# A two-block transformer on one core: second attention in another order, softmax joined over a step, set-up of the recurrence moved

## The chip, the cores and the metric

The kernel runs on one core of a Trainium2 chip. The metric is the device time of one execution in microseconds (us). A core has a matrix engine (TensorE, PE in the profile), a vector engine (VectorE, DVE), a scalar engine (ScalarE, ACT), a general one (GpSimd, POOL) and a queue engine for transfers (SyncE, SP). Each runs its own list of instructions strictly in order, and semaphores make one wait for another.

## The reference

256 tokens of width 1024 go through two blocks. The first block has two attention layers, each followed by a gated per-layer embedding (PLE):

```python
def first_block(x, p, ...):
    for i in range(DEPTH):                       # DEPTH = 2
        h = rms_norm(x, norm_gain[i])
        x = x + (moba_layer if i % 2 == 0 else nsa_layer)(h, ...)
        gate = jax.nn.sigmoid(rms_norm(x, ple_gate_gain[i]) @ ple_w_gate[i])
        x = x + gate * (p[i] @ ple_w_proj[i])
    return x

def nsa_layer(h, w_in, ...):
    q, kc, vc, ks, vs, kw, vw, gl, z = jnp.split(h @ w_in, offs, axis=-1)
    kc = compress(split_heads(kc, 4), cmp_pe[0], cmp_w1[0], cmp_w2[0])
    vc = compress(split_heads(vc, 4), cmp_pe[1], cmp_w1[1], cmp_w2[1])
    ...
    g = jax.nn.sigmoid(gl).reshape(B, T, N_HEADS, 3).transpose(0, 2, 1, 3)
    o = merge_heads(nsa_attention(q, kc, vc, ks, vs, kw, vw, g)) * jax.nn.silu(z)
    return o @ w_out
```

The first attention (MoBA) is plain causal attention at this length (one block of 256 keys), 16 heads of 64. The second (NSA) adds three branches for every head, each scaled by its own sigmoid gate: attention over compressed keys (`compress`: windows of 32 tokens, an MLP of width 256), over selected blocks and over a window; with 256 tokens the last two are both causal attention over all keys, with different keys and values. The second block has two layers; each starts with three mixers in parallel (a state-space recurrence `s5_mixer`, latent attention and a gated linear recurrence), then cross attention and a gated MLP. The recurrence's parameters (step sizes, complex exponentials, bounds) depend on the weights alone.

## The kernel before, in words

Everything is float32. A matrix product `x @ w` splits both operands into a high and a low part and runs three products per block of 128 rows: high by high, low by high, high by low (`dense`, L493 to L495, with the weight streaming as 512 columns; `mm_T`, L507 to L509, with the activations streaming as 256 columns). `weights` (L463 to L478) fetches a weight tile by a transfer on SP's queue, casts it to `whi` on ACT (L476) and forms `wlo` on DVE (L477). `hilo` (L394, L396, L397) does the same to activations.

Attention runs in steps (`attention`, `step`). A two-bank step takes heads of even and of odd number into two PSUM banks: products for the scores (`score`, L1003 in NSA), `softmax` for each bank (L577 to L601), transposes of the probabilities on PE with a copy on ACT (`transposed`, L610 and L612), and products with the values (L659). In `softmax`, DVE adds the mask and takes the row maximum (L587), ACT takes the exponential with its sum (L594), DVE inverts the sum (L596), multiplies it by the gate where there is one (L598) and scales the probabilities (L599). `pipeline` keeps one step in flight ahead of the next.

Work that is to lie beside dense products is a generator in a list of background jobs. `spawn(job, rate)` enters it, each weight tile of a dense product calls `tick`, which advances every job by its rate, and `finish` runs a job to its end. In this way the program's order of instructions is made; a scheduler then fixes each engine's list from it.

In `moba` (up to L758) the two halves of the heads are spawned, `swish_T` forms the gate, `ple_proj(0)` multiplies the embedding, the jobs are finished, `gated` multiplies by the gate and splits, and `project` is the output projection, whose result is added to `x` (L528). After it the main program spawns `setup_mix` at rate 0.6 (L1988) and finishes it behind `nsa`. `setup_mix` (L1895) runs `ssm_params`, `hg_bound`, `hg_reset` and `mla_tables`: small transfers on POOL's queue, transposes on PE (L1267) and a long series of DVE instructions on 128x32 tiles: an exponential by a polynomial (L1226 to L1239), reductions of angles (L1245 to L1249, L1283 to L1298) and the coefficients (L1303 to L1353).

In `nsa` the order before is: product for the compressed keys and values (`pc`), `compress_blocks`, queries and keys of half 0, gates, queries of half 1, spawn of half 0's attention, `compress_mlp` for the keys, keys of half 1, spawn of half 1's attention, `compress_keys`, `swish(0)`, `compress_mlp` for the values, `compressed` (scores of the compressed branch L974, its softmax L980 to L990), `swish(1)`, `compress_values` (L919, L922), `compressed_T` (L997), `ple_proj(1)`, the rest of the attention jobs, `blend` (L1021) and the output projection.

Of the kernel before, what the change touches and what calls it, by code (L numbers as in the profile page):

```python
# [14 lines left out]
OP = mybir.AluOpType  # L15
# [28 lines left out]
R_PREP, R_SET = (0.8, 0.4), 0.6  # L44
# [186 lines left out]
class Net:  # L231
# [345 lines left out]
    def softmax(self, own, t, heads, ps, scale, causal, gate):  # L577


        nc = self.nc  # L580
        n, nk = ps.shape[1], ps.shape[2]
        s, mx, sm = own.F(n, nk), own.T(n), own.T(n)
        if causal:
            mask = self.c["tri"][:, 256 - nk:256]
            ops, far = ((OP.add, OP.min), 3e38) if scale == -1.0 else ((OP.subtract, OP.max), -3e38)
            for i in range(n):
                nc.vector.tensor_tensor_reduce(s[:, i, :], ps[:, i, :], mask, 1.0, far, *ops, mx[:, i:i + 1])  # L587
        else:
            nc.vector.reduce_max(mx, ps, axis=AX.X)
        if scale != -1.0:  # L590
            nc.vector.tensor_scalar(mx, mx, -scale, None, op0=OP.mult)
        src = s if causal else ps
        for i in range(n):
# [21 lines left out]
    def attention(self, t, steps, score, scale, v, blocks, end, causal=True, gate=None, joint=1):  # L615
# [16 lines left out]
        def step(gs):  # L632
            own = Scope(self)

            def scores():
# [4 lines left out]
                return [self.softmax(own, t, hs, p, scale, causal, gate) for p, hs in zip(ps, gs)]  # L640

            def turn(ws):
                out = []
                for w in ws:
                    out.append(self.transposed(own, w))
                    own.drop(w)
# [62 lines left out]
    def moba(self, act):  # L709
# [39 lines left out]
        self.swish_T(act, w, 3 * D, sz)  # L749
        proj = self.ple_proj(0)  # L750
# [5 lines left out]
        nxt = self.boundary(self.project(oT, I["moba_w_out"][0], D), self.gain("ple_gate_gain", 0))  # L756
        oT.close()
# [168 lines left out]
    def nsa(self, act):  # L926
# [73 lines left out]
        def attend(g, qT):  # L1000
            def block(t, b):
# [4 lines left out]
                def end(bank):  # L1006
# [3 lines left out]
                    else:  # L1010
# [3 lines left out]
                                      gate=lambda hs: gate[:, t, hs[0]:hs[-1] + 1:2, 1 + b])  # L1014
# [30 lines left out]

        pc = self.dense(act, w, D, 1024, 512)
# [3 lines left out]
        own0, qT0 = queries(0)  # L1050
# [969 lines left out]
```

## Time and profile before

| what | value |
|---|---|
| runs | 1521.4, 1518.18, 1514.51 us; median 1518.18 us |
| profiled execution | 1515.88 us, its span 1514.1 us |
| mean granted clock of PE | 0.991 |
| busy share of the span | PE 96%, PE weight load 83%, DVE 76%, ACT 58%, POOL 3% |
| chain that ended last | PE 73%, DVE 13%, ACT 8%, transfers 3%, issue 3% |

The span reaches from the first to the last instruction of the profiled execution; 1.78 us lie around it. The chain that ended last is followed back from the last instruction, at each step to what released it. A wait is an engine's idle time before an instruction, put down to the engine that released it last. The granted clock is a share of PE's full speed: 1.0 is 2.4 GHz, 0.5 is 1.2 GHz.

### The profile page before, as it was taken

How to read it: one execution, taken by the hardware profiler on the slowest of the kernel's cores; microseconds unless marked ns; L12 is line 12 of the kernel's file. 1: busy time of each engine (PE TensorE's matmuls, PEld its weight loads, DVE VectorE, ACT ScalarE, POOL GpSimd, SP SyncE). 2: the span in 40 equal slices, each digit the busy share in tenths (PEclk: the TensorE clock that was granted, in tenths of full speed). 3: DMA queues.
4: the chain of work that ended last, by engine and by line, in shares of the span. 5: the costliest groups of instructions: out<-in, count | busy, mean ns of one | idle time of the engine just before them, and what ended most of it. 6: DMA issues, size and time to landing. Idle time of an engine off the chain costs nothing.

```text
span 1514.1 us, 25628 instructions
## 1 busy us (share of the span) xinstructions
PE 1451.9 (96%) x9781; PEld 1259.1 (83%) x9781; DVE 1146.0 (76%) x2479; ACT 881.9 (58%) x1646; POOL 45.7 (3%) x80
## 2 busy tenths in 40 slices
PE   7999999999999999999999999989899999999997
PEld 6787777876788988788889999979787888799996
DVE  7886798988999899757786765676996667665556
ACT  5665566776577966445544544568774455644443
POOL 1001000002000000000100000000000000000000
PEclk9999999999999999999999999999999999999999
DMA  6544545513444345455635555434354565356663
GB/s 201 165 141 127 176 135 177 164 38 117 158 119 137 114 140 172 137 194 169 186 112 181 181 169 182 153 117 123 98 181 140 182 208 163 121 184 202 192 183 125
DMA packets 156059, 233.31 MB, mean 154 GB/s; under 512 B 8946, under 2 KB 91680, under 8 KB 155936
## 3 DMA queue, kind: packets, MB, share of 16 engines
q1 hardware_dynamic: 153888, 228.03, 48.7%
q0 software_dynamic: 1440, 2.53, 0.8%
q8 instruction: 77, 1.26, 0.3%
q10 hardware_dynamic: 608, 1.11, 0.2%
q14 instruction: 46, 0.38, 0.1%
HBM read 230.59 MB, written 1.05 MB: 153 GB/s over the span
## 4 chain that ended last, share of the span: by engine, by line
PE 73%; DVE 13%; ACT 8%; DMA 3%; issue 3%; POOL 0%; SPq 0%; ACTq 0%; DVEq 0%; POOLq 0%
PE mm L493 11%; PE mm L494 10%; PE mm L495 10%; PE sq L507 4%; PE sq L508 4%; PE sq L509 4%; DVE wlo L477 3%; ACT whi L476 3%; PE mm L507 3%; PE mm L508 2%; PE mm L1153 2%; PE mm L1152 2%; PE mm L1154 2%; PE mm L509 2%; PE sq L407 1%
## 5 line engine op out<-in xcount | busy, mean ns | idle before, releaser
L476 ACT CAST whi<-raw 128x1024 fp32r<-128x1024 f32 (+3 forms) x442 | 439.4, 1020 | 400.7 <-PE sq L508 94.8
L477 DVE TENSOR_TENSOR wlo<-raw,whi 128x1024 fp32r<-128x1024 f32 (+3 forms) x442 | 514.1, 1184 | 181.5 <-ACT whi L476 180.2
L493 PE MATMUL mm<-whi,rslab 128*128 128x512 f32 (+1 forms) x944 | 372.0, 396 | 6.9 <-DVE tslab L379 2.9
L494 PE MATMUL mm<-whi,rslab 128*128 128x512 f32 (+1 forms) x944 | 369.6, 392 | 0.1
L495 PE MATMUL mm<-wlo,rslab 128*128 128x512 f32 (+1 forms) x944 | 366.8, 390 | 2.8 <-DVE wlo L477 2.8
L493 PEld LDWEIGHTS mm<-whi,rslab 128*128 128x128 f32 x944 | 178.4, 189 | 46.2 <-ACT whi L476 7.1
L495 PEld LDWEIGHTS mm<-wlo,rslab 128*128 128x128 f32 x944 | 178.9, 190 | 39.4 <-DVE wlo L477 5.5
L494 PEld LDWEIGHTS mm<-whi,rslab 128*128 128x128 f32 x944 | 179.1, 190 | 34.8 <-DVE rslab L397 1.5
L508 PE MATMUL sq<-rslab,whi 128*128 128x256 f32 x544 | 153.0, 281 | 1.3 <-DVE rslab L397 1.0
L507 PE MATMUL sq<-rslab,whi 128*128 128x256 f32 x544 | 153.4, 282 | 0.1
L509 PE MATMUL sq<-rslab,wlo 128*128 128x256 f32 x544 | 152.6, 281 | 0.0
L507 PE MATMUL mm<-rslab,whi 128*128 128x256 f32 x448 | 127.0, 286 | 0.3 <-ACT rslab L396 0.3
L509 PE MATMUL mm<-rslab,wlo 128*128 128x256 f32 x448 | 126.1, 282 | 0.4 <-DVE wlo L477 0.4
L508 PE MATMUL mm<-rslab,whi 128*128 128x256 f32 x448 | 125.6, 282 | 0.0
L508 PEld LDWEIGHTS sq<-rslab,whi 128*128 128x128 f32 x544 | 103.0, 189 | 2.7 <-DVE rslab L397 1.9
L507 PEld LDWEIGHTS sq<-rslab,whi 128*128 128x128 f32 x544 | 103.0, 189 | 1.6 <-ACT fslab L1442 0.7
L509 PEld LDWEIGHTS sq<-rslab,wlo 128*128 128x128 f32 x544 | 103.0, 189 | 0.0
L508 PEld LDWEIGHTS mm<-rslab,whi 128*128 128x128 f32 x448 | 84.1, 188 | 1.8 <-issue 1.1
L507 PEld LDWEIGHTS mm<-rslab,whi 128*128 128x128 f32 x448 | 83.9, 188 | 1.8 <-issue 0.7
L509 PEld LDWEIGHTS mm<-rslab,wlo 128*128 128x128 f32 x448 | 84.2, 188 | 1.2 <-DVE wlo L477 0.8
L1153 PE MATMUL mm<-whi,rslab 128*128 128x512 f32 x176 | 68.9, 391 | 0.0
L1152 PE MATMUL mm<-whi,rslab 128*128 128x512 f32 x176 | 68.8, 393 | 0.0
(448 smaller groups left out, 2288.1 us busy)
## 6 DMA issues: line engine op xcount, KB each, us to landing
raw<-in_w_in_dram SPq DMA_DIRECT2D x96, 512.0 KB, 3.8
raw<-in_ffn_w_gate_up_dram SPq DMA_DIRECT2D x88, 512.0 KB, 4.2
raw<-in_ffn_w_down_dram SPq DMA_DIRECT2D x44, 512.0 KB, 4.2
raw<-in_moba_w_in_dram SPq DMA_DIRECT2D x32, 512.0 KB, 4.5
raw<-in_nsa_w_in_dram SPq DMA_DIRECT2D x28, 512.0 KB, 3.7
raw<-in_ple_w_gate_dram SPq DMA_DIRECT2D x16, 512.0 KB, 4.4
raw<-in_ssm_w_glu_dram SPq DMA_DIRECT2D x16, 512.0 KB, 4.2
raw<-in_w_out_dram SPq DMA_DIRECT2D x16, 512.0 KB, 4.4
```

The costliest lines, as they stand in the source:

```text
L407: nc.tensor.transpose(ps[:, j, t * 128:(t + 1) * 128], src[t][:, (k + j) * 128:(k + j + 1) * 128], self.ident)
L476: nc.scalar.copy(hi[:, js], raw)
L477: nc.vector.tensor_sub(lo[:, js], raw, hi[:, js].bitcast(F32))
L493: nc.tensor.matmul(o, act.hi[:, k, ts], wh[:, j, :], start=k == 0, stop=False)
L494: nc.tensor.matmul(o, act.lo[:, k, ts], wh[:, j, :], start=False, stop=False)
L495: nc.tensor.matmul(o, act.hi[:, k, ts], wl[:, j, :], start=False, stop=k == nkb - 1)
L507: nc.tensor.matmul(o, wh[:, k, fs], act.hi[:, k, :], start=k + i == 0, stop=False, skip_group_check=True)
L508: nc.tensor.matmul(o, wh[:, k, fs], act.lo[:, k, :], start=False, stop=False, skip_group_check=True)
L509: nc.tensor.matmul(o, wl[:, k, fs], act.hi[:, k, :], start=False, stop=last, skip_group_check=True)
L1152: nc.tensor.matmul(o, mid.hi[:, j, ts], wh[:, j, ns], start=first, stop=False)
L1153: nc.tensor.matmul(o, mid.lo[:, j, ts], wh[:, j, ns], start=False, stop=False)
L1154: nc.tensor.matmul(o, mid.hi[:, j, ts], wl[:, j, ns], start=False, stop=last)
```

## The change

There are three parts. **Softmax**: `softmax` takes all banks of a step at once; the reciprocal, the gate product and the scaling are done once for both banks (one 128x1024 operation in place of two of 128x512). **Set-up**: `setup_mix` is spawned inside `moba`, between `swish_T` and `ple_proj(0)`, at rate 1.0, and finished at the end of `moba`. **Order of `nsa`**: gates, queries and keys of both halves come first and each half's attention is spawned as soon as its keys are there; the compressed branch's product, blocks, MLPs, scores and values follow, with `swish(0)` and `swish(1)` ahead of each MLP.

```diff
-R_PREP, R_SET = (0.8, 0.4), 0.6
+R_PREP, R_SET = (0.8, 0.4), 1.0
...
-    def softmax(self, own, t, heads, ps, scale, causal, gate):
+    def softmax(self, own, banks, scale, causal, gate):
...
-        n, nk = ps.shape[1], ps.shape[2]
-        s, mx, sm = own.F(n, nk), own.T(n), own.T(n)
+        m, n, nk = len(banks), banks[0].shape[1], banks[0].shape[2]
+        s, mx, sm = own.F(m, n, nk), own.T(m, n), own.T(m, n)
+        for j, ps in enumerate(banks):
...
             for i in range(n):
-            nc.scalar.activation(s[:, i, :], src[:, i, :], AF.Exp, bias=mx[:, i:i + 1], scale=scale,
-                                 accum_out=sm[:, i:i + 1])
+                nc.scalar.activation(s[:, j, i, :], src[:, i, :], AF.Exp, bias=mx[:, j, i:i + 1], scale=scale,
+                                     accum_out=sm[:, j, i:i + 1])
         nc.vector.reciprocal(sm, sm)
         if gate is not None:
-            nc.vector.tensor_mul(sm, sm, gate(heads))
-        nc.vector.tensor_mul(s, s, sm[:, :, None].to_broadcast([128, n, nk]))
+            nc.vector.tensor_mul(sm, sm, gate)
+        flat = lambda a: a.rearrange("p m n k -> p (m n) k") if len(a.shape) == 4 else a.rearrange("p m n -> p (m n)")
+        nc.vector.tensor_mul(flat(s), flat(s), flat(sm)[:, :, None].to_broadcast([128, m * n, nk]))
...
         self.swish_T(act, w, 3 * D, sz)
+        setup = self.spawn(self.setup_mix(), R_SET)
         proj = self.ple_proj(0)
...
         nxt = self.boundary(self.project(oT, I["moba_w_out"][0], D), self.gain("ple_gate_gain", 0))
+        self.finish(setup)
...
+        gate = sc.F(NT, 16, 3)
+        gates()
+        own0, qT0 = queries(0)
+        keys(0)
+        jobs = [self.spawn(attend(0, qT0), R_NSA[0])]
+        own1, qT1 = queries(1)
+        keys(1)
+        jobs.append(self.spawn(attend(1, qT1), R_NSA[1]))
         pc = self.dense(act, w, D, 1024, 512)
         s1 = Scope(self)
         kk = [self.compress_in(s1, pc, c, act) for c in range(2)]
         blocks = self.compress_blocks(kk[0], 0, pe)
-        own0, qT0 = queries(0)
-        keys(0)
-        gate = sc.F(NT, 16, 3)
-        gates()
-        own1, qT1 = queries(1)
-        jobs = [self.spawn(attend(0, qT0), R_NSA[0])]
+        swish(0)
...
         self.compress_mlp(blocks, 0, gT[0])
         blocks = self.compress_blocks(kk[1], 1, pe)
         s1.close()
-        keys(1)
-        jobs.append(self.spawn(attend(1, qT1), R_NSA[1]))
         self.compress_keys(gT[0], w2, rope[3], kcB)
-        swish(0)
+        swish(1)
         self.compress_mlp(blocks, 1, gT[1])
...
         compressed(1, qT1, pcm[1])
-        swish(1)
         self.compress_values(gT[1], w2, vbd)
...
         act, proj = net.moba(act)
-        setup = net.spawn(net.setup_mix(), R_SET)
         act = net.ple(0, act, proj, net.gain("norm_gain", 1))
         act, proj = net.nsa(act)
-        net.finish(setup)
```

Instructions on each engine: DVE has 48 fewer, PE, ACT and POOL as many as before. Line numbers of the changed file lie up to two higher (L1226 is L1228 there, L997 is L999, L612 is L614).

The change moves instructions on the engines. Ahead of the first attention's output projection, DVE's list before ran from the split of the embedding (`hilo`, L394) to the first gated operand (L397) with three weight splits between:

```order
L394 TENSOR_TENSOR rslab<-sq_1218,rslab 128x512
L477 TENSOR_TENSOR wlo_1322<-raw_1323,whi_1321 128x1024
L477 TENSOR_TENSOR wlo_1322<-raw_1327,whi_1321 128x1024
L477 TENSOR_TENSOR wlo_1356<-raw_1357,whi_1355 128x1024
L397 SCALAR_TENSOR_TENSOR rslab<-fslab,rslab 128x512 x2
L477 TENSOR_TENSOR wlo_1356<-raw_1361,whi_1355 128x1024
```

Now 79 rows stand between that L394 and the first L397 (one of them for four equal instructions); these are the last of them, set-up for the most part:

```order
L1308 TENSOR_SCALAR tslab<-tslab 128x32
L1316 TENSOR_TENSOR tslab<-tslab,ssm_prm 128x32
L1312 TENSOR_TENSOR tslab<-tslab 128x32
L1327 SCALAR_TENSOR_TENSOR fslab<-fslab 128x32
L477 TENSOR_TENSOR wlo_1489<-raw_1494,whi_1488 128x1024
L1313 RECIPROCAL tslab<-tslab 128x32
L1315 TENSOR_TENSOR tslab<-tslab,ssm_prm 128x32
L1588 TENSOR_TENSOR tslab<-tslab 128x4
L397 SCALAR_TENSOR_TENSOR rslab<-fslab,rslab 128x512
L1317 TENSOR_TENSOR tslab<-tslab 128x32
L1589 TENSOR_TENSOR hg_lbt<-tslab 128x4
L397 SCALAR_TENSOR_TENSOR rslab<-fslab,rslab 128x512
```

The 78 set-up instructions between are those of `ssm_params`, `hg_bound` and `mla_tables`, and they came behind the output projection before.

In the second attention's tail, PE's list before had the compressed branch's scores (L974) among swish's products (L507 to L509):

```order
L509 MATMUL mm_3195<-rslab,wlo_3186 128x256
L507 MATMUL mm_3195<-rslab,whi_3185 128x256
L974 MATMUL sq_3062<-fslab 128x64 x8
L974 MATMUL sq_3080<-fslab 128x64 x8
L1003 MATMUL sq_3158<-fslab 128x256
L1003 MATMUL sq_3157<-fslab 128x256
L1003 MATMUL sq_3158<-fslab 128x256
L1003 MATMUL sq_3157<-fslab 128x256
L659 MATMUL po_3177<-fslab 64x256 x4
L508 MATMUL mm_3195<-rslab,whi_3185 128x256
```

The transposes of its probabilities (L997) came 42 rows later. Now the scores (L976), the compressed values' products (L921) and the transposes (L999) follow one another, behind the last MLP, with four products of an attention step (L659) between:

```order
L612 MATMUL sq_3331<-cst,fslab 128x128 x4
L612 MATMUL sq_3337<-cst,fslab 128x128 x4
L885 MATMUL sq_3349<-cst,fslab 128x68 x2
L976 MATMUL sq_3354<-fslab 128x64 x8
L976 MATMUL sq_3372<-fslab 128x64 x8
L921 MATMUL sq_3390<-fslab 128x64
L659 MATMUL po_3449<-fslab 64x256 x4
L921 MATMUL sq_3390<-fslab 128x64 x7
L999 MATMUL sq_3405<-cst,fslab 128x128 x4
L999 MATMUL sq_3411<-cst,fslab 128x128 x4
L407 MATMUL sq_3418<-cst,fslab 128x128 x4
```

Swish's products stand ahead of all of these now.

## Rows read from the trace of the kernel before

**Rows 1.** The page: busy time of each engine, its share of the span, instructions

```profile
PE 1451.9 (96%) x9781; PEld 1259.1 (83%) x9781; DVE 1146.0 (76%) x2479; ACT 881.9 (58%) x1646; POOL 45.7 (3%) x80
```

**Rows 2.** Windows by stage: us, busy time (instructions) of each engine, granted clock, DMA

```profile
164.00:189.00 25.00, 25.00 (x119) 20.19 (x119) 20.89 (x60) 15.56 (x27) 0.00 (x0) 1.00 0.53 174
189.00:258.00 69.00, 63.86 (x320) 50.47 (x319) 63.16 (x221) 43.77 (x66) 1.12 (x4) 1.00 0.54 159
258.00:319.00 61.00, 58.66 (x443) 49.59 (x442) 55.59 (x196) 47.69 (x132) 0.17 (x1) 1.00 0.44 130
319.00:364.00 45.00, 42.72 (x279) 31.51 (x278) 38.30 (x121) 29.40 (x81) 2.80 (x3) 0.96 0.24 77
```

**Rows 3.** Windows: 180 to 240 us, columns as in rows 2

```profile
180.00:240.00 60.00, 56.50 (x270) 44.79 (x269) 58.23 (x225) 37.43 (x63) 0.95 (x2) 1.00 0.49 144
```

**Rows 4.** Timeline of DVE, 130 to 142 us: start, us, line, operation [idle before]

```profile
130.05 0.69 DVE L599 TENSOR_TENSOR fslab<-fslab,tslab 128x512 f32<-128x512 f32 x1
130.66 0.68 DVE L394 TENSOR_TENSOR rslab<-sq,rslab 128x512 fp32r<-128x512 f32 x1
135.78 2.36 DVE L477 TENSOR_TENSOR wlo<-raw,whi 128x1024 fp32r<-128x1024 f32 x2 [4.43 <-ACT whi L476]
139.14 1.22 DVE L477 TENSOR_TENSOR wlo<-raw,whi 128x1024 fp32r<-128x1024 f32 x1 [1.00 <-ACT whi L476]
140.64 1.29 DVE L397 SCALAR_TENSOR_TENSOR rslab<-fslab,rslab 128x512 fp32r<-128x512 f32 x2 [0.28 <-ACT rslab L396]
```

**Rows 5.** Timeline of PE: the first attention's output projection begins

```profile
139.64 1.10 PE L659 MATMUL po<-fslab 128*64 128x128 f32 x16 [1.00 <-ACT fslab L612]
140.67 0.73 PE L493 MATMUL mm<-whi,rslab 128*128 128x512 f32 x2
141.39 0.50 PE L494 MATMUL mm<-whi,rslab 128*128 128x512 f32 x1
```

**Rows 6.** Timeline of DVE: set-up instructions in a chain, and mixed

```profile
177.95 0.18 DVE L1226 TENSOR_SCALAR tslab<-ssm_prm 128x32 f32<-128x32 f32 x1
178.17 0.18 DVE L1227 TENSOR_SCALAR tslab<-tslab 128x32 f32<-128x32 f32 x1
...
178.71 1.22 DVE L477 TENSOR_TENSOR wlo<-raw,whi 128x1024 fp32r<-128x1024 f32 x1
179.85 0.18 DVE L1230 SCALAR_TENSOR_TENSOR tslab<-tslab 128x32 f32<-128x32 f32 x1
...
192.11 0.19 DVE L1234 SCALAR_TENSOR_TENSOR ssm_r<-ssm_r,tslab 128x32 f32<-128x32 f32 x1
...
193.59 0.18 DVE L1237 TENSOR_SCALAR ssm_r<-ssm_r 128x32 f32<-128x32 f32 x1
193.68 1.23 DVE L477 TENSOR_TENSOR wlo<-raw,whi 128x1024 fp32r<-128x1024 f32 x1
```

**Rows 7.** Windows around a PE stall, columns as in rows 2

```profile
378.00:381.00 3.00, 0.02 (x1) 0.00 (x0) 1.02 (x5) 1.05 (x2) 0.00 (x0) 1.00 0.46 153
381.00:385.00 4.00, 3.40 (x12) 3.01 (x13) 4.00 (x9) 2.07 (x6) 0.00 (x0) 0.57 0.15 38
```

**Rows 8.** Timeline of PE: the second attention's tail

```profile
318.05 3.68 PE L974 MATMUL sq<-fslab 128*128 128x64 f32 x32
...
322.72 1.08 PE L659 MATMUL po<-fslab 128*64 128x256 f32 x8
...
335.56 1.58 PE L997 MATMUL sq<-cst,fslab 128*128 128x128 f32 x8
...
338.26 1.55 PE L919 MATMUL sq<-fslab 128*128 128x64 f32 x12
```

**Rows 9.** Timeline of DVE: the compressed branch's softmax and values

```profile
322.97 1.27 DVE L982 TENSOR_REDUCE tslab<-fslab 128x16 f32<-128x512 f32 x2
324.16 1.28 DVE L983 TENSOR_TENSOR fslab<-fslab,tslab 128x512 f32<-128x512 f32 x2
...
325.70 1.27 DVE L985 TENSOR_REDUCE tslab<-fslab 128x16 f32<-128x512 f32 x2
326.89 0.37 DVE L986 RECIPROCAL tslab<-tslab 128x16 f32<-128x16 f32 x2
...
339.85 1.42 DVE L922 TENSOR_TENSOR fslab<-sq,cst 128x256 f32<-128x256 f32 x4 [0.78 <-PE sq L919]
```

**Rows 10.** Groups by form, ACT: exponentials of banks of two heads

```profile
L594 ACT ACTIVATE fslab<-fslab,tslab 128x256 f32<-128x256 f32 x64 | 31.9, 503 | 3.5 <-DVE tslab L587 3.1
```

More of the change, by code (lines that the diff above doesn't have):

```diff
@@ L575, in heads @@
         return [p[:, off:off + nh * 64].rearrange("p (h d) -> p h d", d=64) for p in ps]
-    def softmax(self, own, t, heads, ps, scale, causal, gate):
+    def softmax(self, own, banks, scale, causal, gate):
         nc = self.nc
-        n, nk = ps.shape[1], ps.shape[2]
-        s, mx, sm = own.F(n, nk), own.T(n), own.T(n)
-        if causal:
-            mask = self.c["tri"][:, 256 - nk:256]
-            ops, far = ((OP.add, OP.min), 3e38) if scale == -1.0 else ((OP.subtract, OP.max), -3e38)
-            for i in range(n):
[L587 to L593, printed above, removed]
-            nc.scalar.activation(s[:, i, :], src[:, i, :], AF.Exp, bias=mx[:, i:i + 1], scale=scale,
-                                 accum_out=sm[:, i:i + 1])
+        m, n, nk = len(banks), banks[0].shape[1], banks[0].shape[2]
+        s, mx, sm = own.F(m, n, nk), own.T(m, n), own.T(m, n)
+        for j, ps in enumerate(banks):
+            if causal:
+                mask = self.c["tri"][:, 256 - nk:256]
+                ops, far = ((OP.add, OP.min), 3e38) if scale == -1.0 else ((OP.subtract, OP.max), -3e38)
+                for i in range(n):
+                    nc.vector.tensor_tensor_reduce(s[:, j, i, :], ps[:, i, :], mask, 1.0, far, *ops, mx[:, j, i:i + 1])
+            else:
+                nc.vector.reduce_max(mx[:, j], ps, axis=AX.X)
+            if scale != -1.0:
+                nc.vector.tensor_scalar(mx[:, j], mx[:, j], -scale, None, op0=OP.mult)
+            src = s[:, j] if causal else ps
+            for i in range(n):
+                nc.scalar.activation(s[:, j, i, :], src[:, i, :], AF.Exp, bias=mx[:, j, i:i + 1], scale=scale,
+                                     accum_out=sm[:, j, i:i + 1])
@@ L639, in scores, with turn @@
                         score(p[:, i, :], hs[i], nk)
[L640 to L646, printed above, removed]
+                return self.softmax(own, ps, scale, causal, gate and gate(gs[0][0], len(gs[0])))
+            def turn(w):
+                out = [self.transposed(own, w[:, j]) for j in range(len(gs))]
+                own.drop(w)
                 return out
@@ L1013, in block @@
                                       lambda h, kb: vs[b][:, kb, h // 4, :], (4, 2), end, joint=2,
-                                      gate=lambda hs: gate[:, t, hs[0]:hs[-1] + 1:2, 1 + b])
+                                      gate=lambda h, n: gate[:, t, h:h + 2 * n, 1 + b].rearrange("p (i u) -> p u i", u=2))
             yield from self.pipeline((st for b in range(2) for t in range(NT) for st in block(t, b)), LEAD)
```

## The prediction

> **What bounds the kernel now.** I read the page first. TensorE (PE) is busy 96% of the 1514.1 us span [rows 1], so time is to be had or lost only where PE stands idle or runs at the lower clock. The change touches only the stages between the first attention's last step (about 125 us) and the second attention's output projection (about 364 us); from there on the two programs' PE orders read almost alike. So the windows of that stretch come next [rows 2]: PE is busy in all of 164 to 189 us, for 63.86 of the 69 us of the second attention's first part, for 58.66 of 61 us in its middle and for 42.72 of 45 us in its tail. Idle time is 5.1, 2.3 and 2.3 us, and the tail also has a mean granted clock of 0.96, which is 0.04 x 45 = 1.8 us more. That is all that a better order can win here: 11.5 us. In the first part VectorE (DVE) is what is full: 58.23 of 60 us between 180 and 240 [rows 3], because the set-up of the recurrence parameters runs there, over 100 small instructions.
>
> Around the first attention's output projection it is the other way round. DVE runs `hilo` (L394) at 130.66 us and then waits 4.43, 1.00 and 0.28 us before it forms the first gated operand (L397) at 140.64 us [rows 4]. The output projection's first two products, which need the high part alone, start on PE at 140.67 us, and the first that needs L397's low part (L494) at 141.39 us [rows 5]: there is no slack.
>
> **The set-up, moved.** By the order on DVE, 78 small instructions and four `wlo` splits now stand between L394 and the first L397; before there were three splits. Seven more small ones stand just ahead of L394. What one costs there is not in the trace at this place, so I bound it from where the set-up runs now [rows 6]. In a strict chain they start 0.22 us apart (177.95 to 178.17); where two or three chains are mixed, 16 of them take 1.57 us (192.11 to 193.68), 0.098 each. The new rows are mostly mixed and chained at the start, and I take a quarter at 0.22 and the rest at 0.098, so 0.13. A `wlo` takes 1.14 us from start to start (178.71 to 179.85 in the same view, and half of 2.36 us in [rows 4]). So L397 comes at 131.3 (end of L394) + 0.7 (the seven) + 78 x 0.13 + 4 x 1.14 = 146.7 us in place of 140.64: the output projection is **6.1 us late**. Bounds: with 0.098 it is 3.5 us, with 0.22 it is 13.2 us. Nothing covers it: ahead of that product PE has only the steps of the attention that it finishes anyway, and its order there has no other dense work left.
>
> An idle PE of this length has a second price. In the profile, after the 3 us in which PE did 0.02 us of work, the next 4 us have a granted clock of 0.57 [rows 7], which is mostly 1.2 GHz in place of 2.4, so 0.43 x 4 = **1.7 us**. Bounds 0 and 3.4 (twice).
>
> The set-up leaves 177 to 221 us. PE loses 5.1 us in the window that holds this [rows 2]; I take back 4.6 us of it (**-4.6**; bounds 0 and -5.1), since the first part is now dense work for queries, keys and gates with a relieved DVE. The parameters' small loads on GpSimd's queue go ahead of the second attention's gain loads; those wait behind the position load, which waits for a DVE result of the set-up. I cost this at nothing: they are needed only in the second attention. The gates' and compression weights' loads on SyncE's queue trade places with equal loads: nothing.
>
> **The second attention, reordered.** The attention steps begin earlier and lie under swish and both compression MLPs: the middle can win at most its 2.3 us. Against this DVE has to do most of the attention in that stretch, and where DVE was that full PE lost 60 - 56.50 = 3.5 us in 60 [rows 3]. I put 0 (bounds -2.3 and +4).
>
> The tail is where PE's order binds. Before, the compressed branch's scores (L974) run at 318.05 us and the transposes of its probabilities (L997) at 335.56 us [rows 8]; the 17.5 us between are filled with swish's products and attention steps. Now, by the order, PE has between them only the second half of the scores (1.84 us), the compressed values' products (2.1 us for 16 like the 12 of 1.55) and one group of four L659 (0.54 us): 4.5 us. Meanwhile DVE and ACT must do the compressed softmax for both halves [rows 9]: L980, L982, L983, L985 and L990 twice each at 0.60 from start to start (6.0), L986 and four tiny ones (0.7), two copies and four products of the values (2.0), and one joint 128x1024 product (1.2): about 10 us. PE waits the rest, **5.6 us**, at L997's successor, L999, and everything behind it waits too, as PE runs its list in order; its clock then falls as above (**1.7 us**). The old tail's 2.3 us of idle time and 1.8 us of clock go away in exchange (**-4.1**). Net **+3.2**. Bounds: -4.1 if the chain hides, +7.3 if the old waits stay.
>
> **The joint softmax.** Per two-bank step (18 of them) one reciprocal, one gate product and one scaling of 128x1024 stand for two each. Two L599 take 2 x 0.61 from start to start (130.05 to 130.66 in [rows 4]), one 128x1024 operation 1.14; with the small ones a step saves about 0.3 us of DVE, 18 x 0.3 = 5 us in all, where DVE has room nearly everywhere: I put 0 (bounds -2 and +6.4). The price is that the first bank's transposes wait for the second bank's exponentials too: two at 0.50 us each [rows 10] and half the product, 1.6 us per step, hidden while another step is in flight. The Trainium skill, "Perfetto Trace Analysis", section "Optimizing Scalar/DVE Operations", speaks against this edit here: where DVE and ScalarE are not saturated but hold up other engines, it advises smaller instructions so that work is done sooner. By that rule the sum would be higher by what the last rival below gives.
>
> **Sum.** 6.1 + 1.7 - 4.6 + 0 + 3.2 + 0 = +6.4 us. The profiled execution took 1515.88 us, so **1522.3 us**. That execution lies 2.3 us under the median of the three runs, 1518.18, and within their spread of 1514.51 to 1521.4; I add nothing for it.
>
> **The rivals.**
> A, *the cover wins* (faster). The set-up's instructions mix perfectly (3.5 us late, PE's clock stays up), the first part wins all of 5.1, the middle 2.3, and the compressed chain hides in attention steps that are late anyway, so the old tail's 4.1 goes: 3.5 - 5.1 - 2.3 - 4.1 = -8.0, 1507.9 us. For it: the second attention's dense work now surrounds all of its steps. Against it: the order in the tail, and L397 behind 78 instructions.
> B, *the set-up is a chain* (slower). DVE starts its 78 instructions 0.22 us apart: 13.2 us in place of 6.1, total +13.5, 1529.4 us. It decides the sign from 0.145 us apart on, where the sum passes +7.6. For it: the exponential's polynomial and the angle reductions are chains, each instruction reading the one before. Against it: the mixed stretch in [rows 6].
> C, *little happens*. The late L397 costs 3.5 us without a clock drop, the relief returns 4.6, the tail gives and takes the same: -1.1, 1514.8 us. That the change does not do what it says is excluded by the order, where the set-up and the compressed branch stand in their new places.
> D, *joining exposes the first bank*. In the tail's last four steps, where no step behind covers, the transposes wait 1.6 us longer each: +6.4 on top of the sum, 1528.7 us. The Trainium skill's sentence above is this mechanism. For it: in the old tail PE already waits for ACT's and DVE's softmax results. Against it: in the new tail fewer steps are left.
>
> **Chances.** A measurement of this kernel can tell about 0.5%, 7.6 us, from no change. Forecast 0.40, of which 0.17 lies above +7.6 (its sum is 1.2 us below that bound); A 0.30, of which 0.25 passes -7.6; B 0.11; C 0.14; D 0.05. So faster 0.25, within 0.5% 0.23 + 0.05 + 0.14 = 0.42, slower 0.17 + 0.11 + 0.05 = 0.33. The range reaches from 1505 (A less the 2 us that the joint softmax can give, and rounded down) to 1532 (B plus the 1.7 us by which the clock's bound lies over its value, and rounded up); about 2 in 10 lie outside.
>
> **What would show it.** In the new profile DVE has no idle time between L394 and the first L397, PE a gap of about 6 us ahead of the first attention's output projection with a lower granted clock behind it; PE is nearly full from 180 us to the first scores of the second attention; a PE wait of 5 to 6 us stands before the transposes of the compressed probabilities, in a tail without swish. If PE's order there shows no such waits, the sum is wrong by these terms; if the middle shows PE idle for more than 4 us beside a full DVE, the term that I put at 0 was the one that mattered.

## The result and the profile after

The changed kernel took 1531.54 us (median of 5 runs, 1528.80 to 1534.82) beside 1518.94 us for the kernel before (5 runs, 1514.51 to 1521.52): a ratio of 1.0085, with a 95% interval of 1.0056 to 1.0113. It is slower by 12.6 us, beyond the 0.5% that a measurement of this kernel can tell. The forecast was 1522.3 us in a range of 1505 to 1532.

The page of the changed kernel: busy time of each engine [rows 1].

```profile
PE 1457.6 (95%) x9781; PEld 1265.4 (83%) x9781; DVE 1144.9 (75%) x2431; ACT 883.1 (58%) x1646; POOL 45.6 (3%) x80
```

PE's busy time rose by 5.7 us and its idle time from 1514.1 - 1451.9 = 62.2 to 1527.0 - 1457.6 = 69.4 us. The mean granted clock over the span fell from 0.991 to 0.986: 1514.1 x 0.009 = 13.6 us were lost to the clock before, 1527.0 x 0.014 = 21.4 us now. Idle time and clock each grew by some 7 us (idle time at half rate counts in both).

DVE's timeline around the first attention's output projection, from `hilo` to the first gated operand [rows 4]:

```profile
131.51 0.69 DVE L394 TENSOR_TENSOR rslab<-sq,rslab 128x512 fp32r<-128x512 f32 x1
132.11 0.18 DVE L1232 SCALAR_TENSOR_TENSOR tslab<-tslab 128x32 f32<-128x32 f32 x1
...
136.31 1.22 DVE L477 TENSOR_TENSOR wlo<-raw,whi 128x1024 fp32r<-128x1024 f32 x1
...
144.12 1.23 DVE L477 TENSOR_TENSOR wlo<-raw,whi 128x1024 fp32r<-128x1024 f32 x1
...
145.63 0.69 DVE L397 SCALAR_TENSOR_TENSOR rslab<-fslab,rslab 128x512 fp32r<-128x512 f32 x1
```

DVE's timeline has no wait between L394 and the first L397, which starts at 145.63 us, 5.0 us later than before. PE's timeline there [rows 5]:

```profile
140.78 0.73 PE L493 MATMUL mm<-whi,rslab 128*128 128x512 f32 x2 [0.50 <-ACT rslab L396]
146.38 0.80 PE L494 MATMUL mm<-whi,rslab 128*128 128x512 f32 x1 [4.87 <-DVE rslab L397]
146.97 0.63 PE L495 MATMUL mm<-wlo,rslab 128*128 128x512 f32 x1
147.40 0.63 PE L493 MATMUL mm<-whi,rslab 128*128 128x512 f32 x1
...
152.09 0.43 PE L493 MATMUL mm<-whi,rslab 128*128 128x512 f32 x1
152.37 0.40 PE L494 MATMUL mm<-whi,rslab 128*128 128x512 f32 x1
```

PE waits 4.87 us for that operand. Behind the wait 13 products, to 152.09 us, start 0.43 us apart, and then 0.23 us. The windows of the same place and of the second attention (us, busy time and instructions of PE, PEld, DVE, ACT and POOL, granted clock, DMA) [rows 2]:

```profile
146.00:152.00 6.00, 5.62 (x13) 4.47 (x14) 6.00 (x32) 1.26 (x2) 2.88 (x5) 0.50 0.50 111
189.00:262.00 73.00, 70.81 (x350) 54.87 (x350) 60.77 (x160) 44.01 (x86) 0.00 (x0) 1.00 0.53 157
262.00:340.00 78.00, 74.45 (x572) 62.49 (x570) 65.49 (x190) 64.66 (x168) 1.64 (x5) 1.00 0.38 113
340.00:372.00 32.00, 26.84 (x160) 20.61 (x160) 22.86 (x51) 15.79 (x31) 1.90 (x2) 0.89 0.30 95
```

The first addition to `x` (L528) starts at 157.90 us in place of 151.06. From 189 to 262 us PE is idle for 2.2 of 73 us (5.1 of 69 before), with DVE at 60.77; from 262 to 340 us it is idle for 3.55 of 78 (2.3 of 61). The tail has 5.2 us idle in 32 and a clock of 0.89. PE's timeline in the tail [rows 8], in which the waits stand where the order put them:

```profile
345.49 3.79 PE L976 MATMUL sq<-fslab 128*128 128x64 f32 x32
...
352.13 1.98 PE L921 MATMUL sq<-fslab 128*128 128x64 f32 x14 [1.61 <-DVE fslab L918]
356.41 1.09 PE L999 MATMUL sq<-cst,fslab 128*128 128x128 f32 x4 [2.31 <-DVE fslab L992]
358.07 1.09 PE L999 MATMUL sq<-cst,fslab 128*128 128x128 f32 x4 [0.58 <-DVE fslab L992]
```

PE waits 1.61 us for a copy on DVE (L918) and 2.31 and 0.58 us for the compressed probabilities (L992).

### The profile page after: what moved, and what is told of

It reads as the page before. It is cut to its first block, busy times and chain, and to the rows that moved or that the text cites. A ratio compares the mean times of both kernels' runs of the same rounds, so it can differ in the third digit from the quotient of the medians.

```text
span 1527.0 us, 25580 instructions
## 1 busy us (share of the span) xinstructions
PE 1457.6 (95%) x9781; PEld 1265.4 (83%) x9781; DVE 1144.9 (75%) x2431; ACT 883.1 (58%) x1646; POOL 45.6 (3%) x80
## 4 chain that ended last, share of the span: by engine, by line
PE 70%; DVE 9%; ACT 8%; DMA 2%; issue 2%; POOL 0%; ACTq 0%; DVEq 0%; SPq 0%; POOLq 0%
PE mm L493 10%; PE mm L494 10%; PE mm L495 10%; PE sq L507 4%; PE sq L508 4%; PE sq L509 4%; ACT whi L476 3%; PE mm L1155 2%; PE mm L1154 2%; PE mm L1156 2%; PE mm L507 2%; PE mm L509 2%; PE mm L508 2%; DVE wlo L477 2%; PE sq L407 2%
## 5 line engine op out<-in xcount | busy, mean ns | idle before, releaser
L494 PE MATMUL mm<-whi,rslab 128*128 128x512 f32 (+1 forms) x944 | 369.4, 392 | 5.4 <-DVE rslab L397 5.3
L494 PEld LDWEIGHTS mm<-whi,rslab 128*128 128x128 f32 x944 | 179.2, 190 | 40.1 <-DVE rslab L397 6.7
L507 PE MATMUL sq<-rslab,whi 128*128 128x256 f32 x544 | 153.4, 282 | 0.1
L509 PE MATMUL sq<-rslab,wlo 128*128 128x256 f32 x544 | 152.6, 280 | 0.0
L507 PE MATMUL mm<-rslab,whi 128*128 128x256 f32 x448 | 128.9, 290 | 0.3 <-ACT rslab L396 0.3
L509 PE MATMUL mm<-rslab,wlo 128*128 128x256 f32 x448 | 127.2, 285 | 0.4 <-DVE wlo L477 0.4
L508 PE MATMUL mm<-rslab,whi 128*128 128x256 f32 x448 | 127.4, 286 | 0.0
L507 PEld LDWEIGHTS sq<-rslab,whi 128*128 128x128 f32 x544 | 103.0, 189 | 1.6 <-ACT fslab L1444 0.7
L509 PEld LDWEIGHTS sq<-rslab,wlo 128*128 128x128 f32 x544 | 103.0, 189 | 0.0
L507 PEld LDWEIGHTS mm<-rslab,whi 128*128 128x128 f32 x448 | 85.4, 192 | 2.3 <-issue 1.2
L509 PEld LDWEIGHTS mm<-rslab,wlo 128*128 128x128 f32 x448 | 85.7, 191 | 1.6 <-DVE wlo L477 1.2
L508 PEld LDWEIGHTS mm<-rslab,whi 128*128 128x128 f32 x448 | 85.7, 192 | 1.5 <-issue 0.7
L1155 PE MATMUL mm<-whi,rslab 128*128 128x512 f32 x176 | 68.9, 391 | 0.0
L1156 PE MATMUL mm<-wlo,rslab 128*128 128x512 f32 x176 | 68.8, 391 | 0.0
```

Source lines behind the costliest of these rows:

```text
L494: nc.tensor.matmul(o, act.lo[:, k, ts], wh[:, j, :], start=False, stop=False)
L507: nc.tensor.matmul(o, wh[:, k, fs], act.hi[:, k, :], start=k + i == 0, stop=False, skip_group_check=True)
L508: nc.tensor.matmul(o, wh[:, k, fs], act.lo[:, k, :], start=False, stop=False, skip_group_check=True)
L509: nc.tensor.matmul(o, wl[:, k, fs], act.hi[:, k, :], start=False, stop=last, skip_group_check=True)
L1155: nc.tensor.matmul(o, mid.lo[:, j, ts], wh[:, j, ns], start=False, stop=False)
L1156: nc.tensor.matmul(o, mid.hi[:, j, ts], wl[:, j, ns], start=False, stop=last)
```

## The experiments

The three parts of the change could be taken apart, except that the new order was not tried without the joint softmax. In the table, x1 and x2 are the starts of the first addition to `x` (L528) of the first and second attention, from each run's profile; the median has 6 to 12 runs (before: 5, changed: 5), and the ratio is to runs of the kernel before on the same chip. The runs were spread over several chips, so ratios are compared below, and medians of two rows only with care.

| run | median us | ratio and interval | x1 | x1 to x2 | x2 to end |
|---|---|---|---|---|---|
| before | 1518.94 | | 151.06 | 223.50 | 1139.5 |
| changed | 1531.54 | 1.0085 (1.0056 to 1.0113) | 157.90 | 223.55 | 1145.6 |
| e1 joint softmax alone | 1520.20 | 1.0011 (0.9992 to 1.0031) | 151.60 | 225.90 | 1141.0 |
| e2 set-up alone | 1520.19 | 1.0015 (0.9998 to 1.0033) | 154.66 | 223.13 | 1137.4 |
| e3 without the set-up's move | 1525.70 | 1.0049 (1.0034 to 1.0064) | 154.88 | 228.35 | 1138.3 |
| e4 set-up behind the gated products | 1519.72 | 1.0014 (0.9998 to 1.0030) | 149.87 | 224.97 | 1143.0 |
| e5 compressed scores early | 1525.16 | 1.0051 (1.0032 to 1.0071) | 159.03 | 223.76 | 1140.5 |
| e6 e4 and e5 together | 1521.17 | 1.0015 (1.0000 to 1.0029) | 151.25 | 224.87 | 1143.3 |
| e7 before, with e4's set-up | 1516.92 | 0.9985 (0.9970 to 1.0001) | 150.37 | 220.29 | 1139.9 |
| e8 PE kept busy in the wait | 1531.21 | 1.0080 (1.0057 to 1.0102) | 159.52 | 223.87 | 1145.2 |
| e9 e4, second swish late | 1525.28 | 1.0030 (1.0011 to 1.0048) | 149.71 | 231.31 | 1142.3 |
| e10 e7 with the joint softmax | 1518.12 | 0.9994 (0.9976 to 1.0013) | 150.09 | 223.97 | 1137.8 |
| e11 changed kernel again | 1530.85 | 1.0069 (1.0047 to 1.0092) | 158.53 | 223.73 | 1142.8 |
| e12 e7 again | 1517.97 | 0.9989 (0.9974 to 1.0005) | 150.22 | 221.20 | 1140.0 |

**e1, the joint softmax alone.**

```diff
...
-                return [self.softmax(own, t, hs, p, scale, causal, gate) for p, hs in zip(ps, gs)]
+                return self.softmax(own, ps, scale, causal, gate and gate(gs[0][0], len(gs[0])))
...
```

The rest of the edit is the new body of `softmax`, as in the change.

> The kernel before with the joint softmax alone (set-up and order of the second attention as before). My theory, that DVE's saving of about 5 us lies beside other work and that a step in flight hides the longer wait: within 3 us of before, no new PE wait above 1 us. The rival that joining exposes the first bank's transposes: 4 to 7 us slower, with longer PE waits at the transposes in the second attention's bare tail (327 to 335 us). The rival that a relieved DVE pays: 2 to 5 us faster.

The ratio is 1.0011, 1.7 us, and its interval takes in 1. My theory holds for the time; not for the waits, since a new one of 1.7 us appears (L919 behind L916). Whether joining costs a little, the interval leaves open.

**e2, the set-up alone.**

```diff
-R_PREP, R_SET = (0.8, 0.4), 0.6
+R_PREP, R_SET = (0.8, 0.4), 1.0
...
         self.swish_T(act, w, 3 * D, sz)
+        setup = self.spawn(self.setup_mix(), R_SET)
...
+        self.finish(setup)
...
-        setup = net.spawn(net.setup_mix(), R_SET)
...
-        net.finish(setup)
```

> The kernel before with the set-up alone moved into the first attention. My theory (the first gated operand stands behind the set-up on DVE, PE waits 5 us and then runs at half clock): about 7 us later at the first x update, 3 to 4 us given back in the second attention's first part where DVE is relieved, so 3 to 4 us slower in all. The rival that the whole loss of the changed kernel comes from the second attention's new order: within 1 us of before or faster.

1.0015, some 2 us, below the 3 to 4 expected. x1 is 3.6 us late, not 7: beside the old softmax 52 small instructions and three splits stand ahead of the first L397 on DVE, where the changed kernel has 78 and four; it starts at 143.07 us, 2.6 us earlier than there, and PE's longest wait for an L397 is 1.7 us. The stage behind x1 is 0.4 us shorter. So this part costs, but alone it costs only about a sixth of the 12.6 us (0.0015 x 1518 = 2.2).

**e3, the changed kernel without the set-up's move** (the diff of e2 taken back).

> The changed kernel with the set-up put back behind the first attention (joint softmax and new order kept). My theory: the first x update is back at 151 us; the set-up fills DVE again while the second attention's first dense products run; the tail's wait at the transposes of the compressed probabilities (2.3 + 0.6 us in the changed kernel) and its low clock stay: 3 to 6 us slower than before, 7 to 9 us faster than the changed kernel. The rival that the new order alone costs it all: as slow as the changed kernel, 12 us over before.

1.0049, 7.4 us over before and 5.5 us (1.0085 - 1.0049) below the changed kernel: between my theory and the rival, and nearer to mine. The stage from x1 to x2 takes 228.35 us, 4.85 more than before. With e1 at 1.0011, the new order costs some 0.0038, 5.8 us, when nothing relieves DVE. x1 was to be back at 151 us and came at 154.88, 3.3 us later than in e1, though the lists of PE, DVE and ACT are the same in both up to the second attention. The reason is in the windows, of e3:

```profile
130.00:137.00 7.00, 5.92 (x24) 4.11 (x25) 2.08 (x4) 1.50 (x5) 0.00 (x0) 0.55 0.29 112
```

and of e1:

```profile
130.00:137.00 7.00, 5.86 (x36) 4.43 (x36) 2.44 (x5) 3.54 (x9) 0.31 (x1) 1.00 0.33 125
```

The granted clock is 0.55 in the one execution and 1.00 in the other, behind the same two waits of PE, 1.1 us (L659) and 1.0 us (L612). So the same short waits can be followed by half rate in one execution and not in another. GpSimd's list and its loads are not the same in these two; the last section has a pair of executions of one and the same program.

**e4, the set-up behind the gated products.**

```diff
         self.swish_T(act, w, 3 * D, sz)
-        setup = self.spawn(self.setup_mix(), R_SET)
         proj = self.ple_proj(0)
...
         act.close()
+        setup = self.spawn(self.setup_mix(), R_SET)
         nxt = self.boundary(self.project(oT, I["moba_w_out"][0], D), self.gain("ple_gate_gain", 0))
```

> The changed kernel with the set-up spawned behind the first attention's gated products, so that on DVE the gated operands stand ahead of it and it lies beside the output projection's products. My theory: the PE wait of 4.9 us ahead of the output projection and the half clock behind it go; 6 to 8 us faster than the changed kernel, 4 to 6 us slower than before (the tail and what follows stay). The rival that the set-up's DVE work is the cost wherever it stands: the waits turn up at the first x updates instead, and it gains less than 3 us on the changed kernel.

1519.72 us, 2 us over before. By the ratios it is 10.8 us faster than the changed kernel (1.0085 - 1.0014) and 8.4 us faster than that kernel's second measurement (e11, 1.0069). The wait of 4.9 us is gone and x1 comes at 149.87, 8.0 us earlier, about the wait and the clock behind it (4.9 + 2.6 = 7.5 us). So my theory has the right place; what goes beyond it lies behind x2 (1143.0 against 1145.6 and 1142.8), where it does not repeat. The set-up as DVE work is not the cost, its place on DVE is.

**e5, compressed scores and softmax ahead of the second swish.**

```diff
+        s1 = Scope(self)
+        pcm = [s1.F(NT, 8, 32) for _ in range(2)]
+        compressed(0, qT0, pcm[0])
+        compressed(1, qT1, pcm[1])
         swish(1)
         self.compress_mlp(blocks, 1, gT[1])
-        s1 = Scope(self)
-        pcm = [s1.F(NT, 8, 32) for _ in range(2)]
-        compressed(0, qT0, pcm[0])
-        compressed(1, qT1, pcm[1])
```

> The changed kernel with the compressed branch's scores and softmax put ahead of the second swish and the second MLP. My theory (in the tail PE waits 1.6 us for a copy and 2.9 us for the compressed probabilities, and its clock falls): the waits at the transposes go, the tail's granted clock rises, 5 to 7 us faster than the changed kernel, that is 1524.5 to 1526.5 us. The rival that the tail is bound by the last attention steps and the values' products anyway: less than 2 us faster.

The median is in the expected range, but the reason does not hold. PE's waits in e5 from 335 to 375 us (engine, line, waited for: us in total, times, longest):

```profile
PE sq L885 <- DVE fslab L813: 1.7, 1, 1.7
PE sq L921 <- DVE fslab L918: 0.8, 1, 0.8
```

The wait for L992 is gone and another has come: PE stands 1.7 us for L813, the MLP's activation for the values. The tail's window, from 340 to 375 us:

```profile
340.00:375.00 35.00, 30.75 (x169) 23.85 (x166) 23.93 (x53) 19.04 (x42) 0.95 (x1) 0.85 0.37 114
```

4.25 us idle in 35 at a clock of 0.85, and x1 to x2 takes 223.76 us as in the changed kernel. In the stage nothing was won, so the rival (the values bind the tail anyway) is right there; the 6 us by which the median is lower do not come from the tail in this profile. They lie behind x2 (1140.5 against 1145.6), about 3 us of them in the first mixer layer, where PE's list is another in e5 (below). By the ratios e5 is 5.2 us faster than the changed kernel, but only 2.7 us faster than e11, and the two intervals overlap.

**e6, both.** (The diffs of e4 and e5.)

> The changed kernel with both: set-up behind the gated products, and the compressed branch's scores and softmax ahead of the second swish. If the two waits are independent, the gains add: e4's 12 us and e5's 5 to 7 us, 1512 to 1515 us, the first version that is faster than before. The rival that the waits are in the same slack and only one of them counts: 1518 to 1520 us, no better than e4.

1.0015 beside e4's 1.0014: the rival holds, nothing is added to e4.

**e7, the kernel before with e4's set-up.** (e4's spawn and its finish on the kernel before, at rate 1.0, with the spawn and finish of before taken out.)

> The kernel before (its softmax and its order of the second attention) with the set-up moved behind the first attention's gated products. It shows what relieving DVE in the second attention's first part is worth without a late gated operand. My theory: the 5.1 us of PE idle there shrink to 1 or 2, nothing is lost at the output projection, 3 to 5 us faster than before, 1513 to 1515 us. The rival that this relief pays only with the new order: within 1.5 us of before.

0.9985. The stage from x1 to x2 is 3.2 us shorter, and of the window 189 to 258 us PE is now idle for 3.8 us instead of 5.1:

```profile
189.00:258.00 69.00, 65.22 (x333) 52.31 (x333) 55.69 (x124) 41.38 (x64) 0.34 (x2) 1.00 0.52 156
```

Less than expected, and the interval just reaches 1. Of the 3.2 us only 1.3 are that idle time.

**e8, PE kept busy in the wait.** The added work is not part of the computation.

```diff
         act.close()
+        pt = self.sq((128, 4, 128))
+        for i in range(50):
+            nc.tensor.transpose(pt[:, i % 4], self.ident, self.ident)
         nxt = self.boundary(self.project(oT, I["moba_w_out"][0], D), self.gain("ple_gate_gain", 0))
```

> The changed kernel with 50 extra 128x128 transposes of a constant on PE, whose result nobody reads, in the wait ahead of the first attention's output projection. They add work and remove no wait: L397 still comes at 145.6 us. My theory (the wait itself costs 5 us, the half clock behind it 2.7 us): the output projection still starts at about 146 us, at a granted clock of 1.0, and the first x update comes 2.4 to 2.7 us earlier than in the changed kernel; 1528 to 1530 us in all. The rival that the slow products behind the wait have another cause than the idle PE (operands or weights that come late): no gain, the products there stay at 0.43 us from start to start.

PE's timeline in e8, the extra transposes (L759) and the products behind them:

```profile
144.16 4.58 PE L759 MATMUL sq<-cst 128*128 128x128 f32 x40
148.50 0.48 PE L493 MATMUL mm<-whi,rslab 128*128 128x512 f32 x1
148.81 0.39 PE L494 MATMUL mm<-whi,rslab 128*128 128x512 f32 x1
149.04 0.39 PE L495 MATMUL mm<-wlo,rslab 128*128 128x512 f32 x1
```

the first gated operand on DVE:

```profile
143.95 0.68 DVE L397 SCALAR_TENSOR_TENSOR rslab<-fslab,rslab 128x512 fp32r<-128x512 f32 x1
```

and two windows:

```profile
126.00:140.00 14.00, 12.13 (x61) 8.77 (x61) 11.01 (x53) 7.40 (x19) 0.74 (x1) 0.76 0.22 77
...
147.00:160.00 13.00, 11.98 (x61) 9.85 (x59) 12.65 (x50) 3.38 (x4) 0.81 (x2) 1.00 0.46 131
```

Behind the filled place the products start 0.23 us apart at a clock of 1.00, where the wait of 4.8 to 4.9 us was followed by slow ones in the changed kernel, in e5 and in e11. That fits an idle PE as their cause; one execution shows it. The time is not better, and two things are in the way. In this execution the half rate fell on the products ahead (0.76 from 126 to 140 us), as in e3. And the wait was not only filled: the first L397 starts at 143.95 us here, 1.7 us earlier than in the changed kernel, since fewer instructions stand ahead of it in DVE's list (52 small ones and two splits), but PE works on the transposes until 148.5 us and so starts the product that needs it (L494) at 148.81, some 4 us after the operand is there. The output projection began 2.4 us later than in the changed kernel, and x1 came at 159.52. What the clock alone is worth in the time could not be read from this run.

**e9, e4 with the second swish behind the compressed scores.**

```diff
-        swish(1)
         self.compress_mlp(blocks, 1, gT[1])
...
         compressed(1, qT1, pcm[1])
+        swish(1)
```

> The changed kernel with the set-up behind the gated products (as in e4) and the second swish moved back behind the compressed branch's scores, so that its 96 products (about 11 us of PE) stand between the scores and the transposes of the compressed probabilities, as they did before. My theory (the stage from the first attention's to the second attention's first x update is 225.0 us in e4 because the tail is bare, and 220.3 in e7): the waits ahead of the transposes go, and the stage takes 220 to 222 us; 3 to 5 us faster than e4, 1515 to 1517 us, below before. The rival that moving dense work only moves the waits (the middle loses what the tail wins): the stage stays at 224 to 226 us and the time within 1.5 us of e4.

A miss for both: the stage takes 231.31 us, 6.3 us more than in e4, and 1.0030 against 1.0014. The longest wait of PE from 150 to 385 us in e9, and the window that it lies in:

```profile
PE mm L874 <- ACT rslab L393: 4.5, 1, 4.5
```

```profile
300.00:320.00 20.00, 11.27 (x64) 7.47 (x63) 13.57 (x45) 11.46 (x32) 1.29 (x3) 0.73 0.30 84
```

Swish was the cover between the first MLP and the second's operands (L393). With it gone PE waits 4.5 us, and the clock falls to 0.73. The dense work covers one place or the other.

**e10, e7 with the joint softmax.** (The diffs of e1 and e7.)

> e7 (the order of before with the set-up behind the gated products) with the joint softmax added. My theory that joining costs and gives nothing: within 2 us of e7, 1515 to 1519 us. The rival that joining delays the first bank's transposes where nothing covers them (the stage from x update to x update was 2.4 us longer in e1 than before): 2 to 4 us slower than e7, with PE waits in the bare tail.

0.9994 against 0.9985 and 0.9989 (e12): joining costs 0.0005 to 0.0009, 0.8 to 1.4 us, less than the intervals can tell. My theory holds, though in this profile the stage is 3.7 us longer than in e7. Beside e4 (1.0014), from which it differs by the second attention's order alone, it is some 3 us faster, with intervals that overlap.

**e11, the changed kernel again.** (No diff.)

> The changed kernel itself once more, to tell what of its loss repeats. In its first profile the stages stood so against before: first x update 6.8 us late, the stage from there to the second attention's first x update equal (223.5 us), everything behind it 6.1 us longer (1145.6 against 1139.5), although PE's order there is almost the same. My theory that the last part is mostly chance of the clock (which stalls are followed by half rate differs from one execution to the next): the first two figures repeat within 2 us, the last one comes out between 1139 and 1144 us. The rival that the change makes the later stages slower by itself: 1145 us or more again.

x1 158.53 and x1 to x2 223.73 repeat. Behind x2 it is 1142.8 us: of the 6.1 us there, 2.8 do not repeat and 3.3 do.

**e12, e7 again.** (No diff.)

> e7 once more (order and softmax of before, set-up behind the gated products), the one version that came out under before: 0.9985, interval 0.997 to 1.0001. If the relief of DVE in the second attention's first part is real (3.2 us in the stage between the x updates in e7's profile), the stage again takes 219 to 222 us and the ratio lies between 0.997 and 0.9995. If e7 was chance of the clock, the stage is at 223 us or more and the ratio at 1.000 or above.

The stage is 221.20 us and the ratio 0.9989: both as the relief would have it. Two measurements lie below 1 by 0.0011 and 0.0015, each with an interval that reaches just over 1: about 2 us faster at best.

## Why the prediction was right, and where its sum was short

The sign and the main mechanism were right, and the time lay inside the range, at its upper end; the sum of +6.4 us is half of the 12.6 measured. That the time lay inside is in part luck: it is 0.5 us below the upper end, which was worked out from rival B, and B's price did not come true. Nor did the chances put a clear loss first (0.33, against 0.42 for no clear change). Two of its sums are a little off (13.2 us for 13.1 in rival B, 5.6 for 5.5 in the tail), which changes nothing.

- **The late operand** (+6.1): PE's product that needs L397 starts 146.38 - 141.39 = 5.0 us later. The 78 small instructions and four splits take 145.63 - 132.11 = 13.5 us, (13.5 - 4.6) / 78 = 0.115 us each, near the 0.13 that was chosen and far from rival B's 0.22. e4 shows that the place decides.
- **The clock behind it** (+1.7): 13 products at 0.43 in place of 0.23 us, 2.6 us; in e11, behind the same wait (4.82 us), it is six products and 1.2 us, so the size differs from one execution to the next. The two terms give 7.6 us where 7.8 was forecast; x1 is 6.8 and 7.5 us late in the two profiles of the changed kernel.
- **The relief of the second attention's first part** (-4.6): mis-sized. The idle time there falls by 2.9 us in the changed kernel. In e7 and e12, where only the set-up moves, it falls by 1.3 us; their whole stage is 3.2 and 2.3 us shorter, and the rest does not lie in this part.
- **The middle** (0): idle 3.55 of 78 in place of 2.3 of 61 us, +1.2.
- **The tail** (+3.2): the waits are 1.6 + 2.3 + 0.6 = 4.5 us (2.9 of them at L999) where 5.6 was forecast at L999 alone, and the clock costs 0.11 x 32 = 3.5 us where 1.7 was; less the old tail's 4.1 that is +3.9. The place was right, and the wait at L999 that was read from the order alone is in the trace. What was wrong is the thought that it binds by itself: in e5 it went, and the wait for the values' MLP took its place.
- **The stage from x1 to x2** as a whole: -4.6 + 0 + 3.2 = -1.4 forecast, +0.1 and +0.2 measured. The three terms as measured in the windows make -2.9 + 1.2 + 3.9 = +2.2; a window of one kernel does not hold quite the work of the other's, so these terms are good to some 2 us. e3 against e1 and e4 against e10 put the cost of the new order at 5.8 and 3 us in the whole time (only the first is clear of the intervals), and the relief gives back about 2 (e7, e12).
- **Behind x2** (0): this is the step that failed. "From there on the two programs' PE orders read almost alike", and so nothing was put there; it is +6.1 us in the first profile and +3.3 in the second. Windows from x2 to the end, of the kernel before, of the changed kernel and of e11:

```profile
374.56:1514.10 1139.54, 1102.67 (x7714) 978.18 (x7712) 834.66 (x1570) 644.91 (x1150) 22.72 (x38) 0.99 0.51 158
381.45:1527.00 1145.55, 1106.65 (x7714) 981.81 (x7712) 834.66 (x1570) 645.03 (x1150) 22.90 (x38) 0.99 0.51 157
382.26:1525.10 1142.84, 1103.64 (x7714) 978.81 (x7712) 835.04 (x1570) 645.14 (x1150) 22.90 (x38) 0.99 0.51 157
```

PE's idle time grows from 36.9 us to 38.9 and 39.2, which repeats. Its busy time, for the same 7714 instructions, grows by 4.0 us in the one profile and by 1.0 in the other, which does not. Two places stand out in both profiles. Around the second attention's output projection DVE waits for a transfer, and PE behind it: 3.63 us in the changed kernel, 3.58 before, 4.29 in e11. DVE's wait in the changed kernel:

```profile
387.14 0.43 DVE L1416 TENSOR_TENSOR fslab<-fslab,ssm_cf 128x256 f32<-128x256 f32 x1 [3.83 <-DMA fslab<-in_ssm_b_im_dram]
```

The clock behind PE's wait is lower: windows of 12 us there, in the changed kernel, in e11 and before

```profile
389.00:401.00 12.00, 12.00 (x47) 9.88 (x46) 9.75 (x22) 4.82 (x9) 0.00 (x0) 0.77 0.33 105
390.20:402.20 12.00, 11.96 (x44) 9.86 (x45) 9.83 (x24) 4.62 (x9) 0.00 (x0) 0.77 0.32 101
382.00:394.00 12.00, 12.00 (x53) 9.98 (x52) 10.69 (x27) 5.19 (x11) 0.00 (x0) 0.90 0.43 141
```

where 0.77 against 0.90 of 12 us is 1.6 us. Whether the change makes this is open: e5 has the same wait (3.6 us) and a clock of 0.88 behind it. And in the first mixer layer PE idles 1.9 us and runs at 0.93 in both profiles of the changed kernel; in the first and the second

```profile
516.60:540.00 23.40, 21.52 (x169) 19.51 (x167) 21.43 (x42) 21.06 (x45) 1.18 (x3) 0.93 0.37 114
514.00:540.00 26.00, 24.13 (x193) 21.98 (x191) 24.28 (x51) 23.61 (x46) 1.33 (x4) 0.93 0.37 108
```

against 0.6 us and 1.00 before:

```profile
508.00:530.00 22.00, 21.38 (x183) 19.73 (x182) 19.64 (x41) 19.85 (x42) 1.11 (x3) 1.00 0.40 122
```

That is 3 us more, and here the orders are not alike. Of some 500 instructions of PE around this place, about 110 stand elsewhere in its list. The largest move is that of 16 matmuls (L1439, L1437 before), which stood behind a run of some 50 dense products (L507 to L509) and directly ahead of the transposes that belong to them (L1441); now they stand ahead of that run. PE's timeline before, and in the changed kernel with the two waits that are new:

```profile
523.30 1.86 PE L1437 MATMUL sq<-fslab 128*128 128x32 f32 x16
525.00 1.07 PE L1441 MATMUL sq<-cst,fslab 128*128 128x128 f32 x8
```

```profile
526.53 1.87 PE L1439 MATMUL sq<-fslab 128*128 128x32 f32 x16
...
529.39 0.33 PE L1443 MATMUL sq<-cst,fslab 128*128 128x128 f32 x1 [0.67 <-ACT fslab L614]
530.13 0.38 PE L509 MATMUL mm<-rslab,wlo 128*128 128x256 f32 x1 [0.41 <-DVE wlo L477]
```

The two waits stand in e11 and e8 too, which have the same list there; the half rate stands in the changed kernel and e11 and not in e8 (1.00). In e5, whose edit lies in the second attention, PE's list of this layer is nearly that of before again (about 20 of the 500 instructions stand elsewhere), and both the waits and the low clock are gone:

```profile
514.00:540.00 26.00, 25.31 (x213) 23.14 (x207) 24.05 (x51) 23.82 (x47) 1.64 (x4) 1.00 0.40 123
```

So an edit in the second attention alone changes the scheduler's list some 140 us further on, and the waits come and go with that list in the five executions compared here (before and e5 without them, the changed kernel, e8 and e11 with them); how the scheduler comes to it was not tried. What is left behind x2 after the two places is 6.1 - 1.6 - 3 = +1.5 us in the first profile and 3.3 - 1.6 - 3 = -1.3 in the second, and so nothing that repeats. Nor does every kernel with the new order lose here: x2 to end is 1137.4 to 1141.0 us in the six profiles with the old order, and 1138.3 to 1145.6 in the eight with the new one.

The rivals: A is out, its cover did not win; B's place was right and its price wrong; C is out for the late operand. D would have cost 6.4 us by its own sum. In the old order joining cost 1.7 us in e1, with an interval up to 1.0031 (4.7 us), and 0.8 to 1.4 us in e10. So there its size is out, while its direction is not: the stage from x1 to x2 is 2.4 us longer in e1 than before, and 3.7 us longer in e10 than in e7. In the new order, for which D was priced, joining was not tried alone. D's mechanism is that of the Trainium skill, "Perfetto Trace Analysis", section "Optimizing Scalar/DVE Operations": where these engines are not saturated but hold up others, smaller instructions may let work be done sooner. No run here shows a gain from that which is clear of noise.

## What to carry to other kernels

An idle engine in a window is not a free place: what is put there stands in its list, and what counts is what waits behind the last instruction of it. Here 78 instructions of 0.115 us cost most ahead of one operand (8 to 11 us, e4 against the changed kernel) and next to nothing beside the products behind it. And a dense product that is moved to cover one wait uncovers another (e9): count both ends of the move in the order before moving. And where a scheduler makes the lists, compare them to the end of the program: here a list some 140 us behind the last edited stage had changed, and it cost 2 to 3 us.

## What the runs showed of the hardware

The cost of a change like this is in part granted clock, and that part is the less certain one. Of the 12.9 us by which the span grew in the first profile, 5.7 are busy time of PE and 7.2 idle time; of the 11.0 us in the second profile (e11), 2.6 and 8.4. A wait of 4.9 us was followed by 6 us at half rate (0.50 from 146 to 152 us, 13 slow products); in e11 the same wait by six slow products. Far behind the edited stages, the same program behind the same wait (PE for L394, 2.01 and 2.03 us) ran at half rate in one execution and at full rate in the other; windows of the 5 us from there, in the changed kernel and in e11:

```profile
1080.00:1085.00 5.00, 5.00 (x26) 4.18 (x26) 4.89 (x10) 4.24 (x6) 0.00 (x0) 0.56 0.41 109
1082.70:1087.70 5.00, 4.58 (x39) 3.96 (x39) 4.89 (x10) 4.22 (x6) 0.21 (x1) 1.00 0.39 107
```

Behind waits of about 1 us it was 1.00 in e1 and 0.55 in e3, which moved x1 by 3.3 us. Identical programs differed by 2.8 us behind x2 (changed kernel and e11), so single profiles of this kernel tell stages apart only beyond some 3 us.
